# Placing the second down weight row at the activations' bytes: start addresses modulo 256 in a float32r decoder trunk

## The chip, the cores and the metric

The kernel runs on one core of one Trainium2 chip. The metric is the device time of one execution in microseconds (us), the median of several runs. Five engines work beside each other: TensorE (PE; its weight loads stand in the profile as PEld), VectorE (DVE), ScalarE (ACT), GpSimd (POOL) and SyncE (SP), which issues most DMAs.

## The reference, cut to what matters

Two decoder layers over 256 tokens of width 1024. Each layer is a SwiGLU block, a token mixer with three kinds of attention, and a second SwiGLU block, each with an RMSNorm before and after it:

```
def swiglu(h, w_gate, w_up, w_down):
    return (jax.nn.silu(h @ w_gate) * (h @ w_up)) @ w_down      # w_gate, w_up: 1024 x 2816; w_down: 2816 x 1024

for layer in range(DEPTH):                                      # DEPTH = 2
    h = rmsnorm(x, g[0])
    x = x + 0.5 * rmsnorm(swiglu(h, ...layer, 0), g[1])
    h = rmsnorm(x, g[2])
    x = x + rmsnorm(token_mixer(h, ...), g[3])
    h = rmsnorm(x, g[4])
    x = x + 0.5 * rmsnorm(swiglu(h, ...layer, 1), g[5])
```

So there are four SwiGLU blocks (called ffn in the kernel) and two mixers. Everything is float32.

## The kernel before, in words

Every large product is made of three matmuls (`mm3`, L407; all of them are recorded at line 385, the helper `mm`). A float32 operand is split into a high part, which TensorE's float32r format holds, and a low part, the rest; the product is high by high, high by low, and low by high. A weight comes by DMA into a `raw` tile of 128 x 1024, ScalarE copies the high part into the first half of a `ring` tile (L294), VectorE subtracts it to get the low part into the second half (L297).

One ffn walks over 11 column pairs j of 256 columns each. There are three kinds of products in it:

- `ga(j, T)`, for the first one or two pairs: a stationary 128-token tile of the activations `xt`, and 256 moving columns of the ring tile (`ps<-ring,xt` in the profile), 24 matmuls for each of gate and up, and for each token half T.
- `gb(j)`, for the other pairs (10 in the first ffn, 9 in each of the other three, 37 in all): the ring tile is stationary, 128 columns of it at a time, and all 256 tokens of `xt` move (`ps<-xt,ring`): 96 matmuls of 256 columns. ScalarE and VectorE turn the result into the h tiles, a high and a low one.
- `down(j, T)`: a 128-token tile of h is stationary and 512 columns of a row of the down weight move (`ps<-ring,h`). A pair has two down rows, c = 0 and c = 1, each in a ring tile of its own. One `down` is 12 matmuls of 512 columns: first the 6 of row 0 (two halves of the output, three matmuls each), then the 6 of row 1. Only for the last pair (j = 10) do the rows alternate by output half.

In the steady part of an ffn the order on TensorE is gb(j), down(j-1, 0), down(j-1, 1), gb(j+1) and so on. Towards the end `LAST_ORDER` puts the downs that were kept back one behind another. The mixer's last product (`out_`) has the same form as `down`, with the `mixed` tiles (also of the h pool) stationary and rows of w_out moving; the mixer's value products have the form of `ga`, its query and key products that of `gb`.

The order of all instructions is computed by a planner (`Program.run`), from durations written in the code, and does not look at addresses.

Where a tile lies inside its slot is set by `Slots.take`. A slot of the h pool or of the ring is 48 columns (three times `PLACE` = 16 floats, 64 bytes) longer than its contents, and the start inside the slot is chosen so that place k begins 64·k bytes behind the place of the activations modulo 256 bytes, whichever slot it is:

```
o = PLACE * ((place - i * (self.places - 1)) % 4)
```

The activation tile `xt` itself begins at byte 1280 of each partition, a multiple of 256, and all its parts, and all parts of a ring or h tile, begin a multiple of 256 bytes behind its start. The places of before are: all weights of `ga`, `gb` and of the mixer's inputs 1; w_out and the `mixed` tiles 0 (`AT_O`); the down rows and the h tiles of pair j both at `AT_D[j % 3]`, so 0, 1 or 2 in turn. In `down` and `out_` the stationary and the moving operand thus have the same place; in `gb` the stationary one is at 1 and the moving one at 0, in `ga` the reverse.

Of the kernel before, what the change touches and what calls it, by code (L numbers as in the profile page):

```python
# [9 lines left out]
F32R = mybir.dt.float32r  # L10
# [57 lines left out]

BASE_PAD = 32
PLACE = 16  # L70
AT_W, AT_X, AT_O = 1, 1, 0
AT_D = (0, 1, 2)


class Slots:
# [168 lines left out]
def trunk(tc, x, norm_gains, w_gate, w_up, w_down, w_in, w_out, dlam, subln, consts, out):  # L244
# [11 lines left out]
    H2 = Slots(P1, "h2", 12, [128, 512], 1, 4)  # L256
# [23 lines left out]
    def half(pieces, cut=2, place=0):  # L280

        h = Half()
        raw, h.ring = Buf(RAW), Buf(RNG, F32R, place)

        def load():
            for view, ap in pieces:
                nc.sync.dma_start(view(raw.t), ap)

        ld = op("DMA", 1.5, load, [prev[0]], [raw], lag=DMA_LAG)
        hi, lo = [], []  # L290
        w = 1024 // cut
        for s in (slice(w * c, w * (c + 1)) for c in range(cut)):
            def fhi(s=s):
                nc.scalar.activation(h.ring.t[0][:, s], raw.t[:, s], AF.Copy)  # L294

            def flo(s=s):
                nc.vector.tensor_tensor(h.ring.t[1][:, s], raw.t[:, s], h.ring.t[0][:, s].bitcast(F32), OP.subtract)  # L297

            hi.append(op("ACT", act_us(w, False), fhi, [ld] + hi[-1:] + last_hi, [raw, h.ring]))
            lo.append(op("DVE", dve_us(w), flo, [hi[-1]], [raw, h.ring]))  # L300
        last_hi[:] = hi[-1:]
        h.ready = lo
        prev[0] = ld
        return h
# [3 lines left out]
    def half_cols(w, c0, place):  # L308
        r = []
        for kh in range(2):  # L310
            ap = w[512 * kh:512 * (kh + 1), c0:c0 + 256].rearrange("(k p) c -> p k c", p=128)
            r.append(half([(lambda t: t.rearrange("p (k c) -> p k c", k=4), ap)], CUT_C, place))
        return r

    def half_row(w, r0, place):
        return half([(lambda t: t, w[r0:r0 + 128, :])], CUT_R, place)
# [221 lines left out]
    def ffn(l, s, xt, na, turn1, g, final, nxt, pre):  # L538

        wg, wu, wd = w_gate[l, s], w_up[l, s], w_down[l, s]  # L540
        tiles = dict(pre)

        def tile_(kind, j):
            if (kind, j) not in tiles:
                if kind == "D":
                    tiles[kind, j] = [half_row(wd, 256 * j + 128 * c, AT_D[j % 3]) for c in range(2)]
                else:
                    tiles[kind, j] = half_cols(wg if kind == "G" else wu, 256 * j, AT_X if j < na else AT_W)
            return tiles[kind, j]

        hb = {}

        def hbuf(j):
            if j not in hb:
                hb[j] = (Buf(H2, F32R, AT_D[j % 3]), Buf(H2, F32R, AT_D[j % 3]))
            return hb[j]

        hdone = {}
# [2 lines left out]
        def ga(j, T):  # L561
            pg, pu, sg = Buf(PS), Buf(PS), Buf(ES)
            og = rows_op(pg, 0, xt, T, tile_("G", j), True)
            a = op("ACT", act_us(256, True), lambda: nc.scalar.activation(sg.t[:, :256], pg.t[:, :256], AF.Silu), [og], [pg, sg])
            ou = rows_op(pu, 0, xt, T, tile_("U", j), True)
            m = op("DVE", dve_us(256), lambda: nc.vector.tensor_tensor(sg.t[:, 256:], pu.t[:, :256], sg.t[:, :256], OP.mult), [ou, a], [pu, sg])
            rows[j, T] = (sg, m)

        def hturn(j, T):
            sg, m = rows[j, T]  # L570
            p = Buf(PS)
            bh, bl = hbuf(j)

            def pe():
                for c in range(2):
                    nc.tensor.transpose(p.t[:, 128 * c:128 * (c + 1)], sg.t[:, 256 + 128 * c:256 + 128 * (c + 1)], ident)  # L576

            def view(t):
                return t.rearrange("p (m t) -> p m t", m=2)

            o = op("PE", 0.22, pe, [m, o_ident], [p, sg])
            o1 = op("ACT", act_us(256, True), lambda: nc.scalar.activation(view(bh.t)[:, :, TS(T)], view(p.t[:, :256]), AF.Copy), [o], [p, bh])
            o2 = op("DVE", dve_us(256), lambda: nc.vector.tensor_tensor(view(bl.t)[:, :, TS(T)], view(p.t[:, :256]), view(bh.t)[:, :, TS(T)].bitcast(F32), OP.subtract),
                    [o1], [p, bh, bl])
            hdone[j, T] = [o2]

        def gb(j):
            sg = Buf(ES)
            a = None
            bh, bl = hbuf(j)  # L590
            for part in range(2):
                p = Buf(PS)
                hs = tile_("GU"[part], j)
                os = []
                for m in range(2):
                    for ks in steps(STEPS_G):
                        def pe(m=m, p=p, hs=hs, ks=ks):
                            for k in ks:
                                wh, wl = wk(hs, k)
                                c = TS(m)  # L600
                                mm3(p.t[:, 256 * m:256 * (m + 1)], wh[:, c], wl[:, c], xt.hi(k, slice(0, 256)), xt.lo(k, slice(0, 256)), m == 0 and k == 0, k == KC - 1)
                        use = [hs[i] for i in sorted({k // 4 for k in ks})]
                        os.append(op("PE", 0.327 * len(ks), pe, os[-1:] + sum(xt.done, []) + sum((h.ready for h in use), []), [p, xt.b] + [h.ring for h in use]))
                if part == 0:
                    a = op("ACT", act_us(512, True), lambda p=p: nc.scalar.activation(sg.t, p.t, AF.Silu), os[-1:], [p, sg])  # L605
                else:
                    m_ = op("DVE", dve_us(512), lambda p=p: nc.vector.tensor_tensor(sg.t, p.t, sg.t, OP.mult), os[-1:] + [a], [p, sg])  # L607
                    o1 = op("ACT", act_us(512, False), lambda: nc.scalar.activation(bh.t, sg.t, AF.Copy), [m_], [sg, bh])  # L608
                    o2 = op("DVE", dve_us(512), lambda: nc.vector.tensor_tensor(bl.t, sg.t, bh.t.bitcast(F32), OP.subtract), [o1], [sg, bh, bl])  # L609
                    hdone[j, 0] = hdone[j, 1] = [o2]  # L610
# [4 lines left out]
        def down(j, T):  # L615
            bh, bl = hbuf(j)
            last = j == NPAIR_FF - 1
            hs = tile_("D", j)
            for pieces in ([[(0, 0), (1, 0)], [(0, 1), (1, 1)]] if last else [[(0, 0), (0, 1)], [(1, 0), (1, 1)]]):
                cs = sorted({c for c, _ in pieces})  # L620
                ns = sorted({n for _, n in pieces})

                def pe(pieces=pieces):
                    for c, n in pieces:
                        o = slice(256 * c + 128 * T, 256 * c + 128 * (T + 1))
                        w = hs[c].ring.t
                        mm3(acc[2 * T + n].t, bh.t[:, o], bl.t[:, o], w[0][:, HALF[n]], w[1][:, HALF[n]], j == 0 and c == 0, last and c == 1)

                o = op("PE", 1.30, pe, hdone[j, T] + sum((done[2 * T + n] for n in range(2)), []) + sum((hs[c].ready for c in cs), []),
                       [acc[2 * T + n] for n in ns] + [bh, bl] + [hs[c].ring for c in cs])  # L630
                for n in (ns if last else range(2)):
                    done[2 * T + n] = [o]
# [467 lines left out]
```

## Time and profile before

| | |
|---|---|
| time, median of 3 runs | 1015.15 us (1014.77 to 1015.66) |
| the profiled execution | 1013.44 us, its span 1011.7 us |
| TensorE busy | 996.0 us, 98% of the span |
| VectorE, ScalarE busy | 632.2 us (62%), 582.3 us (58%) |
| moved by DMA | 182.86 MB, 181 GB/s in the mean |
| chain that ended last | TensorE 89% of the span, 87% at line 385 |

A row that groups matmuls gives the start of the first, and the time from there to the end of the last. Matmuls are pipelined and the recorded time of one reaches over the start of the next ones (281 ns in the mean for 256 columns, 392 ns for 512), so the pace of a group of n is read either from the start of a group to the start of the next one, or from the group's time less the time of one matmul, divided by n - 1.

### The profile page before, as it was taken

How to read it: one execution, taken by the hardware profiler on the slowest of the kernel's cores; microseconds unless marked ns; L12 is line 12 of the kernel's file. 1: busy time of each engine (PE TensorE's matmuls, PEld its weight loads, DVE VectorE, ACT ScalarE, POOL GpSimd, SP SyncE). 2: the span in 40 equal slices, each digit the busy share in tenths (PEclk: the TensorE clock that was granted, in tenths of full speed). 3: DMA queues.
4: the chain of work that ended last, by engine and by line, in shares of the span. 5: the costliest groups of instructions: out<-in, count | busy, mean ns of one | idle time of the engine just before them, and what ended most of it. 6: DMA issues, size and time to landing. Idle time of an engine off the chain costs nothing.

```text
span 1011.7 us, 18113 instructions
## 1 busy us (share of the span) xinstructions
PE 996.0 (98%) x7144; PEld 923.7 (91%) x7144; DVE 632.2 (62%) x1123; ACT 582.3 (58%) x1133; POOL 33.4 (3%) x59
## 2 busy tenths in 40 slices
PE   8999999999999999999999999999999999999997
PEld 6999999898888999999899999999998789999996
DVE  6755544778898745444685555448699776545433
ACT  6654443769996545444665444347899765444431
POOL 1000000100001000000000000002000020000000
PEclk9999999999999999999999999999999999999999
DMA  8976664684335766665577666548733557666531
GB/s 267 334 262 189 187 181 135 202 243 115 105 115 178 249 189 184 191 186 145 170 229 229 189 188 192 161 152 238 211 104 89 148 165 239 181 199 180 161 105 42
DMA packets 157432, 182.86 MB, mean 181 GB/s; under 512 B 6049, under 2 KB 141473, under 8 KB 157218
## 3 DMA queue, kind: packets, MB, share of 16 engines
q1 hardware_dynamic: 157202, 181.43, 59.4%
q8 instruction: 56, 0.92, 0.4%
q14 instruction: 30, 0.25, 0.1%
q10 hardware_dynamic: 144, 0.26, 0.1%
HBM read 180.62 MB, written 1.05 MB: 180 GB/s over the span
## 4 chain that ended last, share of the span: by engine, by line
PE 89%; ACT 6%; DVE 2%; issue 1%; POOL 0%; DMA 0%; DVEq 0%; POOLq 0%; SPq 0%; ACTq 0%
PE ps L385 87%; ACT q L722 2%; ACT ring L294 1%; PE ps L505 1%; ACT e L789 1%; ACT q L738 1%; ACT junk L428 0%; DVE q L726 0%; DMA grow<-in_norm_gains 0%; ACT sn L867 0%; POOL sm L438 0%; DVE q L742 0%; ACT sn L868 0%; PE ps L576 0%; ACT sn L866 0%
## 5 line engine op out<-in xcount | busy, mean ns | idle before, releaser
L294 ACT ACTIVATE ring<-raw 128x512 fp32r<-128x512 f32 (+1 forms) x552 | 367.7, 705 | 329.3 <-issue 233.6
L297 DVE TENSOR_TENSOR ring<-raw,ring 128x512 fp32r<-128x512 f32 (+1 forms) x552 | 414.6, 787 | 200.5 <-ACT ring L294 195.6
L385 PE MATMUL ps<-xt,ring 128*128 128x256 f32 x4320 | 521.5, 281 | 0.0
L385 PEld LDWEIGHTS ps<-xt,ring 128*128 128x128 f32 x4320 | 515.3, 189 | 4.6 <-issue 1.7
L385 PE MATMUL ps<-ring,h 128*128 128x512 f32 x1248 | 296.0, 392 | 0.0
L385 PEld LDWEIGHTS ps<-ring,h 128*128 128x128 f32 x1248 | 230.1, 188 | 46.1 <-issue 0.3
L385 PE MATMUL ps<-ring,xt 128*128 128x256 f32 x1056 | 127.9, 280 | 1.7 <-DVE xt L511 1.7
L385 PEld LDWEIGHTS ps<-ring,xt 128*128 128x128 f32 x1056 | 124.7, 188 | 2.9 <-DVE xt L511 2.3
L607 DVE TENSOR_TENSOR e<-ps,e 128x512 f32<-128x512 f32 x37 | 25.6, 692 | 110.6 <-PE ps L385 110.6
L437 POOL TENSOR_SCALAR sm<-sm 128x1 f32<-128x1 f32 x24 | 15.8, 659 | 927.2 <-ACT junk L428 714.0
L608 ACT ACTIVATE h<-e 128x512 fp32r<-128x512 f32 x37 | 23.2, 627 | 22.7 <-DVE e L607 22.7
L453 DVE TENSOR_TENSOR e<-ps,gpo 128x512 f32<-128x512 f32 x24 | 16.4, 688 | 21.3 <-ACT junk L428 20.9
L385 PE MATMUL ps<-q,q 128*128 128x256 f32 (+3 forms) x128 | 26.2, 298 | 3.6 <-DVE q L727 2.5
L428 ACT ACTIVATE junk<-ps 128x512 bf16<-128x512 f32 x24 | 14.3, 596 | 26.3 <-PE ps L385 25.2
L385 PEld LDWEIGHTS ps<-q,q 128*128 128x128 f32 (+1 forms) x128 | 19.6, 189 | 9.1 <-issue 2.4
L738 ACT ACTIVATE q<-ps 64x256 fp32r<-64x256 f32 x72 | 27.1, 376 | 1.0
L605 ACT ACTIVATE e<-ps 128x512 f32<-128x512 f32 x37 | 21.9, 592 | 7.1 <-PE ps L385 7.1
L609 DVE TENSOR_TENSOR h<-e,h 128x512 fp32r<-128x512 f32 x37 | 25.4, 685 | 0.0
L789 ACT ACTIVATE e<-sn,sm 128x256 f32<-128x256 f32 (+1 forms) x56 | 24.7, 446 | 0.1
L722 ACT ACTIVATE q<-ps 32x256 fp32r<-32x256 f32 x64 | 23.9, 374 | 0.9
L742 DVE SCALAR_TENSOR_TENSOR q<-ps,q 64x256 fp32r<-64x256 f32 x48 | 20.2, 422 | 1.0
L508 ACT ACTIVATE xt<-ps 128x512 fp32r<-128x512 f32 x24 | 13.2, 591 | 11.8 <-PE ps L505 11.7
(86 smaller groups left out, 395.5 us busy)
## 6 DMA issues: line engine op xcount, KB each, us to landing
raw<-in_w_ffn_gate SPq DMA_DIRECT2D x88, 512.0 KB, 4.6
raw<-in_w_ffn_up SPq DMA_DIRECT2D x88, 512.0 KB, 4.8
raw<-in_w_ffn_down SPq DMA_DIRECT2D x88, 512.0 KB, 4.4
raw<-in_w_in SPq DMA_DIRECT2D x40, 512.0 KB, 5.3
raw<-in_w_out SPq DMA_DIRECT2D x16, 512.0 KB, 3.7
raw<-in_w_in SPq DMA_DIRECT2D x16, 256.0 KB, 4.3
gpo<-in_norm_gains SPq DMA_DIRECT2D x6, 512.0 KB, 5.9
gpr<-in_norm_gains SPq DMA_DIRECT2D x5, 512.0 KB, 4.9
```

Of the source, the lines that this page charges most:

```text
L294: nc.scalar.activation(h.ring.t[0][:, s], raw.t[:, s], AF.Copy)
L297: nc.vector.tensor_tensor(h.ring.t[1][:, s], raw.t[:, s], h.ring.t[0][:, s].bitcast(F32), OP.subtract)
L385: nc.tensor.matmul(o, a, b, start=start, stop=stop, skip_group_check=True)
L453: nc.vector.tensor_tensor(y.t, accs[i].t, gv(), OP.mult)
L605: a = op("ACT", act_us(512, True), lambda p=p: nc.scalar.activation(sg.t, p.t, AF.Silu), os[-1:], [p, sg])
L607: m_ = op("DVE", dve_us(512), lambda p=p: nc.vector.tensor_tensor(sg.t, p.t, sg.t, OP.mult), os[-1:] + [a], [p, sg])
L608: o1 = op("ACT", act_us(512, False), lambda: nc.scalar.activation(bh.t, sg.t, AF.Copy), [m_], [sg, bh])
L609: o2 = op("DVE", dve_us(512), lambda: nc.vector.tensor_tensor(bl.t, sg.t, bh.t.bitcast(F32), OP.subtract), [o1], [sg, bh, bl])
L722: nc.scalar.activation(b.t[QB[e], :], p.t[QB[m], :256], AF.Copy, scale=scale)
L738: nc.scalar.activation(bs[b].t[HB[b ^ e], :], p.t[HB[b], :256], AF.Copy, scale=scale)
L742: nc.vector.scalar_tensor_tensor(lo[b].t[HB[b ^ other], :], p.t[HB[b], :256], scale, bs[b].t[HB[b], :].bitcast(F32), OP.mult, OP.subtract)
L789: nc.scalar.activation(e.t[:, SEG[a]], sn.t[:, SEG[a]], AF.Exp, bias=mn.t[:, a:a + 1], scale=-1.0, accum_out=den.t[:, d0 + a:d0 + a + 1])
```

## The change

The start places of some tiles are set differently. The down rows no longer go by j but by c: row 0 of each pair at place 1, row 1 at place 0. All h tiles are at place 1 (a new constant, `AT_H`). w_out's rows and the `mixed` tiles go from place 0 to place 1. The weights of `ga`, `gb` and of the mixer's inputs, the activations and everything else stay.

```
-AT_W, AT_X, AT_O = 1, 1, 0
-AT_D = (0, 1, 2)
+AT_W, AT_X, AT_O = 1, 1, 1
+AT_H, AT_D = 1, (1, 0)
...
-                    tiles[kind, j] = [half_row(wd, 256 * j + 128 * c, AT_D[j % 3]) for c in range(2)]
+                    tiles[kind, j] = [half_row(wd, 256 * j + 128 * c, AT_D[c]) for c in range(2)]
...
-                hb[j] = (Buf(H2, F32R, AT_D[j % 3]), Buf(H2, F32R, AT_D[j % 3]))
+                hb[j] = (Buf(H2, F32R, AT_H), Buf(H2, F32R, AT_H))
```

No instruction is added, removed or moved on any engine, no tile changes its slot, and no wait changes. Of the 1248 matmuls with 512 moving columns, 576 had both operands at place 0, 384 at place 1 and 288 at place 2; now 720 have both at place 1, and 528 have the moving operand at place 0 and the stationary one at place 1. That last relation is also that of the 4320 matmuls of the form of `gb`.

## Rows read from the trace of the kernel before

**Rows 1.** The page: engines, then the granted clock in 40 slices, tenths of full.

```profile
PE 996.0 (98%) x7144; PEld 923.7 (91%) x7144; DVE 632.2 (62%) x1123; ACT 582.3 (58%) x1133; POOL 33.4 (3%) x59
PEclk9999999999999999999999999999999999999999
```

**Rows 2.** Waits of TensorE, longest in total first: us, times, longest us.

```profile
PE ps L385 <- DVE q L727: 2.5, 8, 0.4
PE ps L385 <- DVE xt L511: 1.7, 3, 0.8
```

**Rows 3.** TensorE groups by form: line, names, shapes, count, busy us, mean ns, idle.

```profile
L385 PE MATMUL ps<-xt,ring 128*128 128x256 f32 x4320 | 521.5, 281 | 0.0
L385 PE MATMUL ps<-ring,h 128*128 128x512 f32 x1248 | 296.0, 392 | 0.0
L385 PE MATMUL ps<-ring,xt 128*128 128x256 f32 x1056 | 127.9, 280 | 1.7 <-DVE xt L511 1.7
```

**Rows 4.** Timeline of TensorE in the first ffn: start us, us, what, count.

```profile
42.62 11.47 PE L385 MATMUL ps<-xt,ring 128*128 128x256 f32 x96
53.92 5.62 PE L385 MATMUL ps<-ring,h 128*128 128x512 f32 x24
59.39 11.47 PE L385 MATMUL ps<-xt,ring 128*128 128x256 f32 x96
70.70 5.60 PE L385 MATMUL ps<-ring,h 128*128 128x512 f32 x24
76.13 11.47 PE L385 MATMUL ps<-xt,ring 128*128 128x256 f32 x96
87.44 5.63 PE L385 MATMUL ps<-ring,h 128*128 128x512 f32 x24
92.90 11.47 PE L385 MATMUL ps<-xt,ring 128*128 128x256 f32 x96
```

**Rows 5.** Timeline of TensorE, 31.68 to 37.3 us (the first ffn's first gb).

```profile
31.48 5.83 PE L385 MATMUL ps<-xt,ring 128*128 128x256 f32 x50
```

**Rows 6.** Timeline of TensorE, 226.1 to 231.55 us (the first mixer).

```profile
225.94 5.83 PE L385 MATMUL ps<-xt,ring 128*128 128x256 f32 x50
```

**Rows 7.** Timeline of TensorE, 217.75 to 223.4 us (the first mixer's values).

```profile
217.54 6.05 PE L385 MATMUL ps<-ring,xt 128*128 128x256 f32 x50
```

**Rows 8.** Busy time, granted clock, DMA share and GB/s in two stretches, matmuls on xt.

```profile
31.75:36.75 5.00, 5.00 (x47) 1.00 1.04 371
44.00:49.00 5.00, 5.00 (x45) 1.00 0.84 263
```

**Rows 9.** Timeline of TensorE, 182.58 to 185.30 us (downs at place 0).

```profile
182.37 3.11 PE L385 MATMUL ps<-ring,h 128*128 128x512 f32 x13
```

**Rows 10.** The same, 185.30 to 188.05 us (first down at place 1 behind them).

```profile
185.09 3.15 PE L385 MATMUL ps<-ring,h 128*128 128x512 f32 x13
```

**Rows 11.** The same, 188.06 to 190.78 us (second down at place 1).

```profile
187.85 3.11 PE L385 MATMUL ps<-ring,h 128*128 128x512 f32 x13
```

**Rows 12.** The same, 190.79 to 193.55 us (first down at place 2).

```profile
190.57 3.16 PE L385 MATMUL ps<-ring,h 128*128 128x512 f32 x13
```

**Rows 13.** Timeline of TensorE at the start of the second ffn.

```profile
336.73 5.69 PE L385 MATMUL ps<-ring,xt 128*128 128x256 f32 x48
348.08 4.39 PE L385 MATMUL ps<-ring,h 128*128 128x512 f32 x18
352.31 11.47 PE L385 MATMUL ps<-xt,ring 128*128 128x256 f32 x96
```

**Rows 14.** VectorE's and ScalarE's weight splits by form: count, busy us, mean ns, idle.

```profile
L297 DVE TENSOR_TENSOR ring<-raw,ring 128x512 fp32r<-128x512 f32 x448 | 288.9, 686 | 85.4 <-ACT ring L294 81.0
L297 DVE TENSOR_TENSOR ring<-raw,ring 128x1024 fp32r<-128x1024 f32 x104 | 126.3, 1222 | 115.1 <-ACT ring L294 114.7
L294 ACT ACTIVATE ring<-raw 128x512 fp32r<-128x512 f32 x448 | 258.1, 623 | 204.5 <-issue 141.9 <-PE ps L385 42.8 <-ACT ring L294 7.0
L294 ACT ACTIVATE ring<-raw 128x1024 fp32r<-128x1024 f32 x104 | 109.8, 1058 | 124.8 <-issue 91.7 <-PE ps L385 28.5 <-DMA raw<-in_w_ffn_down 4.4
```

## The prediction, made before the changed kernel ran

> **What bounds the kernel now.** I read the page first: TensorE is busy 98% of the span, and its granted clock is above nine tenths in all 40 slices [rows 1]. Then TensorE's waits, where the reader is to look for something to remove and finds nothing: the longest total is 2.5 us [rows 2]. The other engines' idle time costs nothing as long as that holds. So only the pace of the matmuls counts, and the groups by form say which [rows 3]: 4320 + 1056 matmuls of 256 columns, 1248 of 512. Their mean times are no pace, since they overlap; the pace comes from the timeline. In the steady part of an ffn 96 matmuls of a gb go from 59.39 to 70.70 us, 11.31 us or 117.8 ns each, and again from 76.13 to 87.44 [rows 4]. The 24 of a down pair take 5.47 us at place 1 (53.92 to 59.39), 5.43 at place 2 and 5.46 at place 0 [rows 4].
>
> The decisive reading is that the same gb can go faster. The 50 matmuls from 31.48 us take 5.83 us; less the 0.28 us of the last that is 113.3 ns each [rows 5], and the mixer's query and key products of the same form have that pace too [rows 6]. Value products, with the operands' roles exchanged, stand at 6.05 us for 50, 117.7 ns [rows 7]. The granted clock is 1.00, the 2.4 GHz level, in a fast and in a slow stretch, and the DMA share is higher in the fast one [rows 8]; neither explains the slow pace. In gb the stationary operand lies 64 bytes beyond the moving one in both. So there are two paces at one pair of places, and a stretch keeps the one it has: which it gets is decided by what ran before. Behind every down of the steady part it is the slow one [rows 4], also in the second ffn, where products before the down were near the fast pace (48 in 5.69 us, the first of them a late one) and the gb behind it is back at 11.47 us for 96 [rows 13].
>
> How the downs' places enter is seen where several stand behind one another. Two token halves at place 0 follow at 3.11 us for 13, that is 12 steps of 226.7 ns [rows 9]. When both operands step to place 1, the first 12 steps cost 2.76 us in place of 2.72 [rows 10], the next 12 again 2.72 [rows 11], and the step to place 2 costs 2.77 [rows 12]. So a change of place disturbs TensorE for about a dozen matmuls, by some 0.04 us in all, and then it settles. That stays with TensorE alone, since it waits for no engine there [rows 2]. My reading is that weight loads and the moving stream, which run beside each other, disturb each other when they meet in the same bytes modulo 256, and that the stream is then pushed into a phase where they no longer meet, or, in the slow gb, into one where they meet again in every matmul. That is a theory; the rows show paces only.
>
> A rule of the Trainium skill speaks against any effect: the page "SBUF — State Buffer", section "Who interferes with whom", gives TensorE two independent read ports, one for the moving operand and one for weight loads, and says that TensorE never waits on anyone. By that rule no start address would change anything and the time would stay. This trace does not agree: 113.3 against 117.8 ns at the same clock, and 0.04 us at a step of 64 bytes, so I keep it as a rival and not as the forecast.
>
> **The change part by part.** No instruction moves, so the sum has only paces in it.
>
> *gb behind a down.* Before, each gb is entered from a down whose operands have equal places, and for the first gb matmul at least one operand's place relation jumps. Now the last six matmuls of every down have the moving operand at place 0 and the stationary one at 1, just as gb has; nothing jumps at the entry. If those six have settled, weight load and stream go on in the same phase, and gb should start at the fast pace. The gain per gb is 11.31 us [rows 4] less 96 x 113.3 ns = 10.88, so 0.43 us. Of the 37 gb, one is fast already [rows 5]; 36 x 0.43 = 15.5 us. The bounds are 0 and 15.5 us; I take 15.5, since the settled 512-column matmuls stand at 226.7 ns [rows 9], twice the fast pace and not twice the slow one, so a settled stream is in the fast phase.
>
> *Inside the downs.* Each of the 88 downs (44 pairs, two token halves) now has two steps of the moving place: 1 to 0 between its rows, and 0 to 1 at its start. That is 176 steps, fewer by a handful since the last pair's rows alternate differently. Such a step, of one operand alone, is not in the trace. The nearest rows: a step of both by 64 bytes costs 0.04 us over 12 matmuls [rows 10, 12], and entering place 2 from gb costs nothing (24 in 5.43 us, 226.3 ns each) [rows 4]; only six matmuls follow each step, so half of 0.04. I take 0.02 us, 3.5 us in all, with ends 0 and 0.04 us, 0 and 7.0 us. No row is below 226 ns, so I exclude a gain here. What goes: two thirds of the 36 entries from gb cost 0.03 us each (5.46 and 5.47 against 5.43) [rows 4], about 0.8 us; and at the end of each of the four ffns some three steps of place, 4 x 3 x 0.04 = 0.5 us. Net +2.2 us, between -1.3 and +5.7.
>
> *w_out and the mixed tiles at place 1.* Both stay equal to each other, 192 matmuls. What can change is the pace of the value and ga products behind: 2 x 192 value products at 117.7 ns [rows 7] could become fast, 2 x 192 ga products near the fast pace [rows 13] could become slow, each 384 x 4.4 ns = 1.7 us. I take zero, ±1.7 us.
>
> *The copies that write the moved tiles.* As many, in the same forms. VectorE needs for one pair j eight splits of 686 ns and two of 1222 [rows 14], 7.9 us, ScalarE 7.1 us, of 16.3 us of matmuls that are left in the fast case (10.88 + 5.43). That hides them; DMA has moved 371 GB/s for a while [rows 8] and needs six raw tiles of 128 x 1024 float32 per pair, 3.1 MB in 16.3 us, under 200 GB/s. No new bound.
>
> Sum: 1013.44 us of the profiled execution - 15.5 + 2.2 = 1000.1. The median lies 1.7 us above that execution, so 1001.8; I say 1002 us. Its own range is 997 to 1008 us (terms at their ends).
>
> **Rivals.** *Slow gb stays, downs cost little.* For it: 36 of 36 entries from a down are slow at three different places [rows 4], so the slow phase may be what any 512-column stretch leads to. Against it: none of them was entered without a jump. Time: 1015.15 + 2.2 = 1017.4 us, at the low end 1013.9. This also covers that addresses of this kind do nothing, 1015.
>
> *Slow gb stays and the downs never settle (slower).* One mechanism: six matmuls are too few to settle, so each of the 176 steps throws the stream back into the disturbed stretch of rows 10 and 12. Six disturbed matmuls cost up to 0.04 us if the disturbance is front-loaded; 7.0 - 1.3 = 5.7 us, 1020.9 us. It also leaves the gb to a phase that is not settled, so the gain is lost. It decides from about 0.019 us a step, where the sum passes 0.2%. For it: about 12 matmuls were needed where downs follow each other [rows 10, 12]. Against it: entering the downs from gb cost only 0.03 us [rows 4].
>
> *Only some gb become fast.* The phase may depend on what went before, as the mixers show both paces [rows 6, 7]. Half of them: 1015.15 - 7.8 + 2.2 = 1009.6 us.
>
> **How the numbers follow.** All gb fast: 0.48, 1002 us. Some: 0.09, 1009.6. Slow and little cost: 0.23, of which 0.03 lies beyond the bound and 0.20 within it. Slow and unsettled downs: 0.20, around 1019. The bound is 0.2%, 2.0 us, about what a measurement of this kernel can tell from no change. So faster 0.57, same 0.20, slower 0.23. The range 998 to 1019.5 us leaves out the best end of the first case and the worst of the last, some two in ten.
>
> **What the changed profile would show.** Right: gb rows of 96 matmuls with 11.04 us in place of 11.47 (95 x 113.3 ns + 0.28), and the start of one gb to the start of the next pair's closer by 0.4 us. Downs: 24 matmuls in 5.44 to 5.55 us; above 5.56 the steps cost more than I took. Granted clock and waits as before. Wrong: 96 still at 11.47 us means that continuity at the entry is not what sets the pace; a longer wait of TensorE for VectorE's splits would mean that the faster gb ran out of cover.

## The result, and the profile after

The changed kernel takes 1003.53 us (median of 4 runs, 1003.50 to 1003.59), before 1015.11 us (median of the 4 runs beside it). The ratio is 0.9887 with a 95% interval of 0.9875 to 0.9900. The profiled execution took 1003.59 us with a span of 1001.8 us, 9.9 us less than the span of before.

The page's engine line, against [rows 1]:

```profile
PE 986.3 (98%) x7144; PEld 909.8 (91%) x7144; DVE 632.5 (63%) x1123; ACT 582.8 (58%) x1133; POOL 34.3 (3%) x59
```

All of the difference is TensorE's own busy time, 996.0 to 986.3 us; the others stay within 1 us. Its waits are as short as in [rows 2]; the longest is now

```profile
PE ps L385 <- DVE q L727: 2.1, 6, 0.4
```

The granted clock in a stretch of gb is 1.00, as it was before [rows 8] (stretch, busy us and count, clock, DMA share, GB/s):

```profile
44.00:49.00 5.00, 5.00 (x46) 1.00 0.82 267
```

The groups of TensorE by form (count, busy us, mean ns, idle), against [rows 3], show where the time went:

```profile
L385 PE MATMUL ps<-xt,ring 128*128 128x256 f32 x4320 | 505.9, 277 | 0.0
L385 PE MATMUL ps<-ring,h 128*128 128x512 f32 x1248 | 299.7, 394 | 0.0
L385 PE MATMUL ps<-ring,xt 128*128 128x256 f32 x1056 | 129.8, 281 | 1.5 <-DVE xt L511 1.5
```

The form of gb lost 521.5 - 505.9 = 15.6 us; the downs gained 299.7 - 296.0 = 3.7 us, and the ga and value products 129.8 - 127.9 = 1.9 us. Together that is 10.0 us less; the span is 9.9 us shorter. The group of gb's form also holds the mixer's 768 query and key products. The 36 gb behind a down make up 36 x 0.42 = 15.1 us of the 15.6, by the starts shown next.

The steady part of the first ffn on TensorE (start us, us, what, count), against [rows 4]:

```profile
42.81 11.05 PE L385 MATMUL ps<-xt,ring 128*128 128x256 f32 x96
53.70 5.72 PE L385 MATMUL ps<-ring,h 128*128 128x512 f32 x24
59.25 11.05 PE L385 MATMUL ps<-xt,ring 128*128 128x256 f32 x96
70.14 5.72 PE L385 MATMUL ps<-ring,h 128*128 128x512 f32 x24
75.70 11.05 PE L385 MATMUL ps<-xt,ring 128*128 128x256 f32 x96
```

A gb takes 10.89 us from its start to the down's (59.25 to 70.14), 113.4 ns a matmul, in place of 11.31. A down pair takes 5.55 us (53.70 to 59.25) in place of 5.43 to 5.47. What became slower in it is seen in the recorded time of single matmuls, whose minimum, median and maximum in ns the view by tile gives. At the pace of 226.7 ns it is 389 ns. Two stretches of the changed kernel, first the end of row 0, then row 1:

```profile
L385 PE MATMUL ps<-ring,h x3: 389/389/389, 54.4 to 54.8; 128*128 128x512 f32 x3
L385 PE MATMUL ps<-ring,h x4: 394/394/394, 55.3 to 56.0; 128*128 128x512 f32 x4
```

Row 1 has an even pace of its own. From start to start its matmuls are 233.3 ns apart in the trace (233, 233 and 234 in turn), with no settling. That is 6.7 ns more than at equal places, and 528 x 6.7 ns = 3.5 us. Row 0 is disturbed at its start and then settles: its six matmuls in the second token half have uneven recorded times.

```profile
L385 PE MATMUL ps<-ring,h x6: 388/391/397, 56.5 to 57.6; 128*128 128x512 f32 x6
```

A pair with 12 matmuls at 226.7 and 12 at 233.3 ns would take 5.52 us. The other 0.03 us of the 5.55 are the two entries into row 0, an estimated 1.3 us over the 44 pairs.

### The profile page after: what moved, and what is told of

It reads as the page before. It is cut to its first block, busy times and chain, and to the rows that moved or that the text cites. A ratio compares the mean times of both kernels' runs of the same rounds, so it can differ in the third digit from the quotient of the medians.

```text
span 1001.8 us, 18113 instructions
## 1 busy us (share of the span) xinstructions
PE 986.3 (98%) x7144; PEld 909.8 (91%) x7144; DVE 632.5 (63%) x1123; ACT 582.8 (58%) x1133; POOL 34.3 (3%) x59
## 4 chain that ended last, share of the span: by engine, by line
PE 87%; ACT 8%; DVE 2%; issue 1%; POOL 1%; DMA 0%; DVEq 0%; POOLq 0%; SPq 0%; ACTq 0%
PE ps L385 86%; ACT q L722 2%; ACT ring L294 1%; ACT q L738 1%; PE ps L505 1%; ACT e L789 1%; ACT junk L428 0%; DVE q L726 0%; ACT sn L867 0%; ACT sn L868 0%; DMA grow<-in_norm_gains 0%; ACT sn L866 0%; DVE q L742 0%; POOL sm L438 0%; PE ps L576 0%
## 5 line engine op out<-in xcount | busy, mean ns | idle before, releaser
L385 PE MATMUL ps<-xt,ring 128*128 128x256 f32 x4320 | 505.9, 277 | 0.0
L385 PEld LDWEIGHTS ps<-xt,ring 128*128 128x128 f32 x4320 | 499.9, 188 | 5.2 <-issue 1.7
L385 PE MATMUL ps<-ring,h 128*128 128x512 f32 x1248 | 299.7, 394 | 0.0
L385 PE MATMUL ps<-ring,xt 128*128 128x256 f32 x1056 | 129.8, 281 | 1.5 <-DVE xt L511 1.5
```

The costliest lines, as they stand in the source:

```text
L385: nc.tensor.matmul(o, a, b, start=start, stop=stop, skip_group_check=True)
```

## The experiments

All kernels differ from the changed one only in the constants shown (places of the ga and value weights, of w_out with the mixed tiles, of h, and of down rows 0 and 1), unless more is said. In all of them gb has the moving operand at place 0 and the stationary one at 1, except where the text says otherwise. A gb of 96 matmuls at 11.05 us in a timeline row is fast, one at 11.47 slow.

**d_only: the down part alone.**

```
-AT_W, AT_X, AT_O = 1, 1, 1
+AT_W, AT_X, AT_O = 1, 1, 0
```

> The down part of the change alone: w_out and the mixed tiles stay at place 0. Theory (what runs before a 256-column stretch sets its pace): the gb stay fast (113.3 ns), the downs as in the changed kernel (row 1 at 233.3 ns), and the ga products behind the mixer, which became slow in the changed kernel, are fast again: 384 x 4.4 ns = 1.7 us, so about 1001.8 us. Rival (the two parts are not tied, the ga pace is chance): 1003.5 us.

Measured: 1003.60 us (1002.79 to 1003.74), ratio 0.9887 (0.9873 to 0.9902), the same as the changed kernel. The ga and value products keep their slow pace (129.4 us in their group). So w_out and the mixed tiles have no measurable share in the result, and my theory on the ga pace is refuted; the rival held. A gb behind a down, and the group of the ga and value products:

```profile
59.20 11.05 PE L385 MATMUL ps<-xt,ring 128*128 128x256 f32 x96
```

```profile
L385 PE MATMUL ps<-ring,xt 128*128 128x256 f32 x1056 | 129.4, 281 | 1.7 <-DVE xt L511 1.7
```

**rows_same: no row at the activations' place.**

```
-AT_H, AT_D = 1, (1, 0)
+AT_H, AT_D = 1, (1, 1)
```

> Both down rows at place 1, as the h tiles: no row at the activations' place, and no place that goes by j. Theory (gb is fast only behind matmuls at gb's own places): all gb slow at 117.8 ns (+15.5 us), downs at 226.7 ns (299.7 us of TensorE back to about 295.5), about 1015 us. Rival (it is enough that the places no longer change from pair to pair): gb fast and downs at 226.7 ns, about 999.5 us.

Measured: 1013.78 us (1012.95 to 1014.01), 0.9988 (0.9979 to 0.9997). All gb are slow; the downs settle at 226.7 ns. Matmuls of a gb, and of a down pair, by tile:

```profile
L385 PE MATMUL ps<-xt,ring x87: 281/281/281, 59.8 to 69.9; 128*128 128x256 f32 x87
...
L385 PE MATMUL ps<-ring,h x20: 389/389/389, 54.7 to 59.0; 128*128 128x512 f32 x20
```

281 ns for a gb matmul is the slow pace; in the changed kernel it is 276:

```profile
L385 PE MATMUL ps<-xt,ring x91: 276/276/276, 59.8 to 70.0; 128*128 128x256 f32 x91
```

So row 1's place makes the difference between fast and slow gb here, and letting the places no longer go by j brings about 0.1%. The gb of the first ffn that stands ahead of its downs is fast in this kernel, and the one behind its first down pair is slow (the row above). So the downs did not only hand on a pace, they ended one:

```profile
L385 PE MATMUL ps<-xt,ring x37: 276/276/276, 32.8 to 36.9; 128*128 128x256 f32 x37
```

**row0_moved: the two rows exchanged.**

```
-AT_H, AT_D = 1, (1, 0)
+AT_H, AT_D = 1, (0, 1)
```

> The two rows' places exchanged: row 0 at place 0, row 1 at place 1, so the last six matmuls before a gb have equal places. Theory: gb slow, as many down matmuls at 233.3 ns as in the changed kernel, about 1019 us. Rival (one row at place 0 anywhere in the pair is enough): 1003.5 us.

Measured: 1019.13 us (1018.98 to 1019.37), 1.0042 (1.0027 to 1.0057), as the theory had it: 528 slow down matmuls and no fast gb behind a down. The order of the two rows decides.

```profile
53.97 5.72 PE L385 MATMUL ps<-ring,h 128*128 128x512 f32 x24
59.53 11.47 PE L385 MATMUL ps<-xt,ring 128*128 128x256 f32 x96
```

**both_moved: no jump anywhere in the steady part.**

```
-AT_H, AT_D = 1, (1, 0)
+AT_H, AT_D = 1, (0, 0)
```

> Both down rows at place 0, h at place 1: all 1056 down matmuls have the relation of gb. Theory: gb fast; every down matmul at 233.3 ns, 6.7 ns more than at equal places, but no steps inside a down: 1056 x 6.7 = 7.0 us in place of 528 x 6.7 = 3.5 and some 1.5 us of steps, so about 1005.5 us. Rival (the 233.3 ns is the cost of stepping between rows, as the prediction had it): downs settle at 226.7 ns, about 999 us.

Measured: 1011.38 us, and the executions differ about twice as much as those of any other kernel: 1008.64 to 1013.41 us. Ratio 0.9960 (0.9945 to 0.9974). Both theories missed. The profiled execution has fast gb in the first ffn and slow ones in the third:

```profile
42.73 11.05 PE L385 MATMUL ps<-xt,ring 128*128 128x256 f32 x96
53.62 5.76 PE L385 MATMUL ps<-ring,h 128*128 128x512 f32 x24
59.21 11.05 PE L385 MATMUL ps<-xt,ring 128*128 128x256 f32 x96
...
535.07 11.47 PE L385 MATMUL ps<-xt,ring 128*128 128x256 f32 x96
546.38 5.76 PE L385 MATMUL ps<-ring,h 128*128 128x512 f32 x24
551.97 11.47 PE L385 MATMUL ps<-xt,ring 128*128 128x256 f32 x96
```

In each of the four ffns all nine gb behind a down have one pace: the first two ffns are fast and the last two slow here. With no change of place between gb and down, a stretch kept the pace that it came with. So an entry without a jump preserved the pace; it did not make it fast. The eight times fall into two groups, 1008.6 to 1010.0 and 1012.7 to 1013.4 us, about as far apart as nine gb are worth (9 x 0.42 = 3.8 us). That another ffn was fast in the shorter ones is not shown, since the trace of one execution alone was kept. The downs, with the very places of row 1 of the changed kernel, do not have its even pace either: their steps alternate between 231 and 236 ns, the same mean.

```profile
L385 PE MATMUL ps<-ring,h x18: 393/396/398, 54.8 to 58.7; 128*128 128x512 f32 x18
```

**all_zero: the same place for everything.**

```
-AT_W, AT_X, AT_O = 1, 1, 1
-AT_H, AT_D = 1, (1, 0)
+AT_W, AT_X, AT_O = 0, 0, 0
+AT_H, AT_D = 0, (0, 0)
```

> All weights, h tiles, mixed tiles and activations at place 0: both operands of every product have the same place, and no place changes between products. Theory (a stretch keeps the pace it has as long as no place changes; a change of place sets it anew): each ffn runs at one pace from its first gb to its last, and which one may differ from ffn to ffn or from one execution to the next, as with both rows at place 0; downs at 226.7 ns. About 998 us if all are fast, 1013 if none. Rival (gb is fast only with its stationary operand 64 bytes beyond the moving one): all gb slow, 1013 us or more in every execution.

Measured: 1025.31 us (1025.03 to 1025.38), 1.0107 (1.0090 to 1.0124). The theory missed, since no ffn is fast. The rival held, with all gb slow and over 1013 us in every execution, but the pace is a third one: 120 ns with equal places, from 60.28 us to the next down at 71.80 us.

```profile
60.28 11.68 PE L385 MATMUL ps<-xt,ring 128*128 128x256 f32 x96
71.80 4.50 PE L385 MATMUL ps<-ring,h 128*128 128x512 f32 x19
```

In these kernels equal places are thus good for 512 columns (226.7 ns) and bad for 256; with the stationary operand 64 bytes beyond the moving one it is 233.3 ns for 512 columns, and 113.3 or 117.8 for 256.

**rel_jump: row 1 in gb's relation, but everything 64 bytes further on.**

```
-AT_H, AT_D = 1, (1, 0)
+AT_H, AT_D = 2, (2, 1)
```

> h at place 2, down row 0 at place 2, row 1 at place 1: row 1 has the stationary operand 64 bytes beyond the moving one, as in the changed kernel and in gb, but everything 64 bytes further on, so both operands step by 64 bytes at the entry into gb. Theory A (gb is fast when the last six matmuls have its very places): slow again, about 1019 us, as with the rows exchanged. Theory B (the distance of the two operands is enough): 1003.5 us.

Measured: 1002.84 us (1002.78 to 1004.07), 0.9889 (0.9874 to 0.9904). All gb are fast although both operands step by 64 bytes at the entry. Theory A, my explanation in the prediction, falls; theory B held here, until t_split below.

```profile
53.58 5.70 PE L385 MATMUL ps<-ring,h 128*128 128x512 f32 x24
59.12 11.05 PE L385 MATMUL ps<-xt,ring 128*128 128x256 f32 x96
```

Row 1 has the even pace again:

```profile
L385 PE MATMUL ps<-ring,h x4: 394/394/394, 57.9 to 58.6; 128*128 128x512 f32 x4
```

**rel_minus and rel_two: row 1 at the activations' place, the stationary operand elsewhere.**

```
-AT_H, AT_D = 1, (1, 0)
+AT_H, AT_D = 3, (3, 0)      # rel_minus: stationary 64 bytes short of the moving operand
+AT_H, AT_D = 2, (2, 0)      # rel_two: 128 bytes beyond it
```

> h and down row 0 at place 3, row 1 at place 0: the moving operand of row 1 lies where gb's does, and steps there by 64 bytes from row 0, but the stationary one is 64 bytes short of it (modulo 256) instead of beyond it. Theory A: slow gb; row 1 at a pace between 226.7 and 233.3 ns, so 1014 to 1019 us. Theory C (it is the moving operand's step to the activations' place, whatever the stationary one does): gb fast, 1000 to 1004 us.

> h and down row 0 at place 2, row 1 at place 0: the moving operand of row 1 lies where gb's does, with the stationary one 128 bytes beyond it. Theory A: slow gb, 1014 to 1019 us by the pace of row 1. Theory C: gb fast, 1000 to 1004 us.

Measured: rel_minus 1003.93 us (1002.98 to 1004.34), 0.9896 (0.9881 to 0.9910), all gb fast; rel_two 1017.76 us (1017.66 to 1018.41), 1.0034 (1.0021 to 1.0047), all slow. In rel_minus the moving operand steps by 64 bytes from row 0 to row 1, in rel_two by 128. Theory A falls once more with rel_minus, theory C with rel_two. Row 1 of rel_minus does not have the even pace (its recorded times are shown third), so that pace is no condition for a fast gb. Gb behind the downs, first of rel_minus, then of rel_two:

```profile
59.05 11.05 PE L385 MATMUL ps<-xt,ring 128*128 128x256 f32 x96
```

```profile
59.50 11.47 PE L385 MATMUL ps<-xt,ring 128*128 128x256 f32 x96
```

```profile
L385 PE MATMUL ps<-ring,h x4: 388/393/397, 57.9 to 58.6; 128*128 128x512 f32 x4
```

**t_split and ct_split: the stationary operand steps instead.** Both rows at place 1; in t_split the h part of token half 1 is at place 2, in ct_split only its part for row 1. The slot of h is wider for it (a small tile, `pr`, shares the memory of another so that it fits), and in ct_split the copies into h are cut in two.

```
-AT_H, AT_D = 1, (1, 0)
+AT_H, AT_D = 1, (1, 1)
...
-                        o = slice(256 * c + 128 * T, 256 * c + 128 * (T + 1))
+                        o = slice(272 * T + 128 * c, 272 * T + 128 * (c + 1))      # t_split
+                        o = 256 * c + 128 * T + PLACE * (c & T)                    # ct_split
```

> Both down rows at place 1; of the h tiles the part of token half 0 at place 1, that of half 1 at place 2 (a wider slot with 64 bytes between the halves). So the 12 matmuls of down(j, 0) have equal places, and the 12 of down(j, 1), which stand before the next gb, have the stationary operand 64 bytes beyond. Theory (what counts is that the last stretch before a gb has the operands 64 bytes apart, in either sense; equal or 128 bytes apart leads to the slow gb): gb fast; as many matmuls at 233.3 ns as in the changed kernel, but fewer steps, so about 1002.5 us. Rival (a step of the moving operand inside each down is needed): gb slow or mixed, 1010 to 1018 us.

> Both down rows at place 1; of the h tiles only the part of row 1 and token half 1 at place 2, the other three at place 1; so only the last six matmuls before a gb have their operands 64 bytes apart, 264 in all in place of 528. The copies into h are cut in two for it (one more ScalarE and one more VectorE instruction per gb). Theory: gb fast, 264 x 6.7 ns = 1.8 us less in the downs and fewer steps than with the changed kernel: about 1001 us. Rival (six matmuls alone do not set the pace, the 1 to 0 steps did): gb slow, about 1015 us.

Measured: t_split 1016.48 us (1015.38 to 1017.57), 1.0015 (1.0006 to 1.0025); ct_split 1016.64 us (1016.20 to 1017.50), 1.0019 (1.0009 to 1.0028). Gb slow in both (in t_split all but the first of each ffn); the rivals came nearer. The comparison with rel_jump is the sharpest: the matmuls just before the gb have the same places (moving at 1, stationary at 2; twelve of them in t_split, six in ct_split and rel_jump), the gb is the same, and it is slow in the one and fast in the other. What differs is how that stretch was entered: from equal places by a step of the stationary operand in t_split and ct_split, by a step of the moving one in rel_jump. The stretch of t_split has another rhythm, too (alternating 231 and 236 ns in place of an even 233.3):

```profile
59.52 11.47 PE L385 MATMUL ps<-xt,ring 128*128 128x256 f32 x96
```

```profile
L385 PE MATMUL ps<-ring,h x10: 393/396/398, 57.0 to 59.1; 128*128 128x512 f32 x10
```

The first gb behind a down in the second, third and fourth ffn of t_split is an exception. The twelve matmuls before it have the same places and came from the same step, but here their pace is the even one, and the gb is fast. So the step alone does not settle the pace; what stood ahead of it has a part. The twelve matmuls in the second ffn, and the gb behind them:

```profile
L385 PE MATMUL ps<-ring,h x12: 394/394/397, 350.6 to 353.2; 128*128 128x512 f32 x12
```

```profile
353.42 11.05 PE L385 MATMUL ps<-xt,ring 128*128 128x256 f32 x96
```

**x_three: the ga and value weights at place 3.**

```
-AT_W, AT_X, AT_O = 1, 1, 1
+AT_W, AT_X, AT_O = 1, 3, 1
```

> The changed kernel with the moving weights of ga and of the mixer's values at place 3 in place of 1, so that their stationary operand, the activations, lies 64 bytes beyond the moving one and no longer 64 bytes short of it. They are 1056 matmuls, nearly all at 117.8 ns in the changed kernel. Theory (no more than: 64 bytes apart in either sense allows both paces, and what ran before chooses): either as before, 1003.5 us, or all fast, 1056 x 4.4 ns = 4.6 us less, 999 us. Rival (this sense of the distance has a pace of its own): over 1005 us.

Measured: 1001.54 us (1000.98 to 1002.15), 0.9869 (0.9854 to 0.9884). The group of these products goes from 129.8 to 127.0 us; not all of them became fast. The form of gb gives some of it back (505.9 to 507.7 us). The time is between the theory's two figures.

```profile
L385 PE MATMUL ps<-ring,xt 128*128 128x256 f32 x1056 | 127.0, 280 | 1.7 <-DVE xt L511 1.7
```

In this kernel the first ffn's gb ahead of its downs has the slow pace, and the one behind its first down pair the fast one. So the downs did not only hand on a fast pace there, they led to it:

```profile
L385 PE MATMUL ps<-xt,ring x37: 281/281/281, 32.7 to 37.0; 128*128 128x256 f32 x37
```

```profile
42.66 11.05 PE L385 MATMUL ps<-xt,ring 128*128 128x256 f32 x96
```

**joined: rel_jump and x_three in one.**

```
-AT_W, AT_X, AT_O = 1, 1, 1
-AT_H, AT_D = 1, (1, 0)
+AT_W, AT_X, AT_O = 1, 3, 1
+AT_H, AT_D = 2, (2, 1)
```

> The two best so far in one: ga and value weights at place 3; h and down row 0 at place 2, row 1 at place 1 (so the moving operand still steps by 64 bytes from row 0 to row 1 and the stationary one does not). Theory (a step of the moving operand away from equal places leads into the stretch of even 233.3 ns, and that into the fast gb): gb fast; entering place 2 from gb costs nothing, so 0.7 us less than with the changed kernel, and 2.0 us less by the ga weights: about 1000.9 us. Rival (the ga pace hangs on the places of the downs before it, so the gains don't add): 1002 to 1004 us.

Measured: 1000.51 us (1000.12 to 1000.76), 0.9858 (0.9841 to 0.9874), the fastest of all, and 0.3% under the changed kernel in the medians. The gains add, as expected: 126.4 us for the ga and value products, 299.3 for the downs.

```profile
L385 PE MATMUL ps<-xt,ring 128*128 128x256 f32 x4320 | 506.1, 277 | 0.0
L385 PE MATMUL ps<-ring,h 128*128 128x512 f32 x1248 | 299.3, 394 | 0.0
L385 PE MATMUL ps<-ring,xt 128*128 128x256 f32 x1056 | 126.4, 279 | 1.5 <-DVE xt L511 1.5
```

## Why the prediction was right, and where its reasons were not

- *What bounds the kernel.* Right. No wait of TensorE grew to matter, and the whole difference lies in the pace of TensorE's matmuls. The faster gb found its cover: the copies and DMAs stayed hidden, and TensorE's longest wait in total is 2.1 us after 2.5 before.
- *All gb become fast, -15.5 us.* Right in outcome and size (-15.6 us in the group, 15.1 of them from the 36 gb behind a down). The reason given, that nothing jumps at the entry into gb, is refuted. With rel_jump both operands jump and the gb is fast; with both_moved nothing jumps and the gb has the pace that the ffn happened to start with. The argument that downs at 226.7 ns are in the fast phase falls with rows_same, where they have that pace and the gb behind them is slow. So it was in part luck that all gb became fast: the change held a step that the prediction had priced as a cost alone, that of the moving operand between the rows. What held of the theory is its other half: a stretch of matmuls carries a state from one product to the next, and a change of place can alter it.
- *What stands in its place.* In every kernel in which all gb behind a down were fast (the changed kernel, d_only, rel_jump, rel_minus, x_three, joined) the moving operand alone steps by 64 bytes from equal places, between row 0 and row 1, and the stationary one stays. No step inside the downs (rows_same), a step that leads to equal places instead of away from them (row0_moved), a step of 128 bytes (rel_two) and a step of the stationary operand alone (t_split, ct_split) gave slow gb in the steady part. The step has to stand between the down's own matmuls: in rows_same and row0_moved the very step of the changed kernel stands at the entry into gb, and the gb is slow. That is a pattern over these kernels and no rule, since the first gb behind a down in three ffns of t_split is fast without it. Why the pace changes stays open. That weight loads and the moving stream meet in the same bytes modulo 256 remains an argument: no view shows the meeting itself.
- *Steps inside the downs, +2.2 us net.* The size was too small (+3.7 us) and the mechanism right for one kind of step alone. I priced 176 steps at 0.02 us, each a disturbance that dies away. For the step back into row 0 that holds: two of them cost 0.03 us a pair, about 1.3 us in all. The step into row 1 is no passing disturbance: an even 6.7 ns on each of the 528 matmuls of row 1, 3.5 us, with no settling in any of its six. That is 0.04 us a step, the upper end of what I allowed. Settled 512-column matmuls go at 226.7 ns at equal places alone. A slip in the sum changes nothing: the terms at their ends give 1007 us at the top, not 1008.
- *w_out and the mixed tiles, zero.* Their share is zero within the noise, as d_only shows. Yet the ga and value products take 1.9 us more, about what I had as a bound (±1.7), and d_only shows the same without any change in w_out: it comes from the change in the downs. By which step of the chain was not tried.
- *The rival from the Trainium skill.* The page "SBUF — State Buffer", section "Who interferes with whom", gives TensorE two independent read ports and says it never waits on anyone. By that rule the changed kernel and the twelve of the experiments would take the time of before. The runs do not agree: with nothing but start addresses changed the time goes from 1000.5 to 1025.3 us.

## What to carry to other kernels

When TensorE is busy all the time and waits for nobody, compare the pace of equal matmuls at several places of the trace: two paces at a granted clock of 1.00 can mean that something is to be had without removing any work; here it was 1.1%, and 1.4% in the best arrangement. Start addresses modulo 256 bytes of the stationary and the moving operand are then worth a search on the chip, over the sequence of products and not over one product alone, since here the same relation gave both paces, depending on what led into it. Judge such a search by several executions: one arrangement (both_moved) took 1008.6 to 1013.4 us from run to run.

## What the runs showed of the hardware that was not expected

- A pace is remembered: in both_moved all nine gb behind a down of an ffn keep 113.3 or 117.8 ns, and the downs between them (5.59 us from 53.62 to 59.21 us, and 5.59 from 546.38 to 551.97) do not alter it.
- The better distance differed with the moving width: at equal places 226.7 ns for 512 columns (rows_same) and 120 ns for 256 (all_zero); with the stationary operand 64 bytes beyond the moving one 233.3 ns for 512 and 113.3 or 117.8 for 256 (both_moved).
- Stepping the moving operand and stepping the stationary one did not come to the same, even where they led to the same two places (rel_jump 1002.8 us, t_split 1016.5 us and ct_split 1016.6).
